# First layer's head in program order: three engines' queues fixed up to MoBA's queries, the second projection chunk in the scores' PSUM banks, the compression one chunk later

## The chip, the cores and the metric

One core of one Trainium2 chip runs the whole program. The metric is device time in microseconds (us) of one execution. The engines are TensorE (PE), VectorE (DVE), ScalarE (ACT) and GpSimd (POOL); SyncE (SP) issues nearly all DMAs. The profile is one execution in the hardware profiler; its times count from the first instruction of the program.

## The reference

Two decoder layers over 256 tokens of width 1024. A layer norms x, projects it with one wide matrix, feeds three token mixers (MoBA, NSA, FoX), gates and lifts their outputs, merges them and projects back onto x.

```python
h = rms_norm(x, norm_g)
proj = h @ w_in          # mq mk mv mz | nq kc vc ksl vsl kw vw ng nz | fq fk fv ff fz gl
q = apply_partial_rope(rms_norm(split_heads(mq, 6), ...), cos, sin)      # MoBA; the same for k
o_moba = moba_attention(q, k, split_heads(mv, 6))
k_cmp = nsa_compress(kc, gidx, cmp_pe[0], cmp_w1[0], cmp_w2[0])          # silu(flat @ w1) @ w2
v_cmp = nsa_compress(vc, gidx, cmp_pe[1], cmp_w1[1], cmp_w2[1])
o_nsa = nsa_attention(q, k_cmp, v_cmp, cmp_end, ksl, vsl, kw, vw, gates)
o_fox = fox_attention(q, k, v, log_f)
merged = g0 * (o_moba*silu(mz) @ w_up_moba) + g1 * (o_nsa*silu(nz) @ w_up_nsa) + g2 * (o_fox*silu(fz) @ w_up_fox)
return x + merged @ w_out
```

## The kernel before

**Weights.** All weights stream from HBM in tiles of up to 1024 columns (`chunk`, L229). A tile is loaded into one of six `st` buffers by SP (`load`, L246), then split into a high half `wh` (ScalarE, L262) and a low half `wl` (VectorE, L263), one of four buffers each (`wsp`). A dense product is three matmuls in reduced-width float: high by high, high by low, low by high (`mm3`, L286 to L289). `prefetch` and `part` (L265 to L280) emit the split of the tile four ahead of the one that is used next (AHEAD = 4). So a split waits for three things: its load, PE's release of the `wh` and `wl` four tiles back, and its place in ACT's and DVE's queues. A load waits for the `st` buffer six tiles back.

**Chunks of the projection.** In the order of use (ORDER, L1032): "a" (NSA's queries, compression tokens, slc keys and values), "mv", "b" (window keys and values, gates), then "w0" to "w3" (the compression's first matrix in four parts, two tiles of four 256 KB loads in all per part) strewn between "mq" and "mz", and so on. Every other chunk comes in two halves (mv0, mv1) of two tiles each.

**PSUM.** `pacc` has four banks: two row tiles of the chunk that is accumulated, two of the chunk that is evacuated. `pat` has three banks named "at", for transposes and later the scores; `po` has one.

**Order.** PE's order is written by hand: the program emits matmuls, and a planner's clock (`tick`, L199) advances by each matmul's estimated cost. Post-processing units are generators that yield the us after which their next part is due (`post_a` L685, `post_b` L712, `cmp_tokens` L733, `v_post`, `qk_post`); their instructions are emitted where the clock finds them due. On ACT, DVE, POOL and SP the framework's own scheduler orders instructions, by priority and estimated readiness. `first_blocks` (L373) chains the first ones by hand.

**The stage at issue** is `run` (L1079) for layer 0, from the first matmul of "a" to w3. `first_blocks` splits a's four tiles together with the first blocks of x; `mm_first` multiplies them; mv follows. Meanwhile x is loaded (L126), squared (L422), and `rsqrt` (L306) makes the row factor `rt` from the sums. All evacuations need rt: `post_a` evacuates kv and vsl (L442), squares the heads (L446, one `sq` buffer) and reduces (L447), makes the head factors, scales and ropes the heads (L511, L464 to L467), the slc keys (L520). `cmp_tokens` transposes kv on PE (L739), adds positions (`zf`, one buffer, L742) and splits the sum into Z (L748 on ACT, L749 on DVE); w0's matmuls (L773, L774) read Z. `rope_tables` (L426) and `cmp_zeros` (L751) are POOL's.

Of the kernel before, what the change touches and what calls it, by code (L numbers as in the profile page):

```python
# [9 lines left out]
F32 = mybir.dt.float32  # L10
# [8 lines left out]
NT = S // 128  # L19
# [74 lines left out]
def trunk(ctx, tc, x, w_in, b_gate, cmp_w1, w_up_moba, w_up_nsa, w_up_fox, w_out, gains_d, eye_d, x_t, small_d, row_d, out):  # L94
# [5 lines left out]
    LAG_T, LAG_C, LAG_A, LAG_F, LAG_Q = 3.5, 4.5, 11.0, 9.0, 10.0  # L100
    HEADS, STAG, SECOND, LAG_S, LAG_P, LAG_B, PV = 2, 2.0, 1.5, 4.5, 2.5, 3.0, 0.1
    ctx.enter_context(tc.manual_schedule(engines={mybir.EngineType.PE}))

    const = ctx.enter_context(tc.tile_pool(name="const", bufs=1))
    lay = ctx.enter_context(tc.tile_pool(name="lay", bufs=1))
# [54 lines left out]
    def late_consts():  # L160
        V.memset(ones1, 1.0)
        G.memset(zer, 0.0)
        for s in (0, 64):
            V.memset(gcol[s:s + 16, 0:12], 1.0)
# [12 lines left out]
    def after(i, others):  # L177

        for o in others:
            tc.add_manual_dep(i.ins, o.ins.name, nosync, reason="one table set after the other")  # L180
# [110 lines left out]
    def new_acc():  # L291
        return [pacc.tile([128, 512], F32, name="acc") for _ in range(NT)]
# [57 lines left out]
    def layer(l):  # L350
# [22 lines left out]
        def first_blocks():  # L373


            last = {}

            def put(e, i):
                after(i, [last[e]] if e in last else [])
                last[e] = i  # L380
            z = sh["z"][0][:, 0:256]
            put(V, V.memset(z, 0.0))
            ps = pat.tile([128, 512], F32, name="at")
            for _ in range(6):
                T.matmul(ps[:, 0:256], z[:, 0:128], z, start=True, stop=True)
            for k in range(KD):
                w_, i = parts[f"a{k // 4}"][k % 4]
                if i == 0:
                    room(w_)
                xt, h, lo = [a[:, k % 4, :] for a in (sh["xt"][k // 4], *sh["hT"][k // 4])]  # L390
                g = ngc[:, l * KD + k:l * KD + k + 1]
                wh, wl = split(w_, i * 512, i * 512 + 512)
                if k == 0:
                    put(V, V.tensor_scalar(h, xt, g, None, op0=ALU.mult))
                else:
                    put(A, A.activation(h, xt, AF.Copy, scale=g))
                put(A, wh())
                put(V, V.scalar_tensor_tensor(lo, xt, g, h.bitcast(F32), op0=ALU.mult, op1=ALU.subtract))
                put(V, wl())
            used[0] = 4  # L400

        def x_loads():

            sh["xt"] = [pgs.tile([128, 4, S], F32, name="xt", tag="page") for _ in range(2)]

            def xk(a, b):
                nc.sync.dma_start(sh["xt"][a // 4][:, a % 4:a % 4 + b - a, :], x_t[:, a:b, :])
            xk(0, 1)
            load(tiles[0], (nc.scalar, nc.sync))
            xk(1, 2)  # L410
            xk(2, 3)
            load(tiles[1], (nc.scalar, nc.sync))
            xk(3, 4)
            xk(4, 6)
            load(tiles[2], (nc.sync,))
            xk(6, 8)
            for w_ in tiles[3:6]:
                load(w_, (nc.sync,))

        def start_r():  # L420
# [20 lines left out]
        def evac(ps, t, col, n, dst):  # L441
            A.activation(dst, ps[t][:, col:col + n], AF.Copy, scale=sh["r"][:, t:t + 1])  # L442
# [6 lines left out]
        def head_factors(ss, nh):  # L449

            rr = sm.tile([128, NT, 8], F32, name="rr")[:, :, 0:nh]
            rsqrt(rr, ss[:, :, 0:nh], 1.0 / HD, (128, NT, nh))
            V.tensor_tensor(rr, rr, sh["r"][:, :, None].to_broadcast([128, NT, nh]), op=ALU.mult)
            return rr
# [70 lines left out]
        def new_ss():  # L525
            return sm.tile([128, NT, 8], F32, name="ss")
# [158 lines left out]
        def post_a():  # L685
            ps = sh["ps_a"]
            sh["nqT"] = lay.tile([128, 2, S], F32, name="nqT")
            sh["nqs"] = lay.tile([128, NH, S], F32R, name="nqs")
            for n in ("kh2", "kl2"):
                sh[n] = lay.tile([128, 2, S], F32R, name=n)  # L690
            sh["kv"] = lay.tile([128, NT, 128], F32, name="kv")
            sh["vsl"] = lay.tile([128, NT, HD], F32, name="vsl")
            ss = new_ss()
            for t in range(NT):
                evac(ps, t, 256, 128, sh["kv"][:, t, :])
                sumsq(ss, ps, t, 0, 4)
                sumsq(ss, ps, t, 384, 1, h0=4)
                evac(ps, t, 448, HD, sh["vsl"][:, t, :])
            rr = head_factors(ss, 5)
            qs = heads_scaled(ps, rr, 0, 4, "nq")  # L700
            ks = shared_scaled(ps, 384, rr, 4, "ns")
            yield LAG_A
            for t in range(NT):
                p3, g = q_cols(qs[t], sh["nqs"], t, 2, "nq")
                A.activation(sh["nqT"][:, :, t * 128:(t + 1) * 128], p3, AF.Copy, scale=g)
                yield 0.2
            yield 3.0
            for t in range(NT):
                shared_cols(ks[t], 0, t, "ns")
                yield 0.2  # L710
# [288 lines left out]
        def mm_out(parts, between):  # L999
# [18 lines left out]
            for t in range(NT):  # L1018
                for n in range(2):
# [9 lines left out]
        parts = {}  # L1029
        PROJ = {"a": (C_NQ, 512), "b": (C_KW, 396), "mq": (C_MQ, 384), "mk": (C_MK, 384), "mv": (C_MV, 384),  # L1030
                "mz": (C_MZ, 384), "fq": (C_FQ, 384), "fk": (C_FK, 384), "fv": (C_FV, 384), "fz": (C_FF, 390)}
        ORDER = ["a0", "a1", "mv0", "mv1", "b0", "w0", "b1", "mq0", "w1", "mq1", "w2", "mz0", "mz1", "w3",  # L1032
                 "mk0", "mk1", "fv0", "fv1", "fq0", "fq1", "fz0", "fz1", "fk0", "fk1"]

        def queue_loads():
# [13 lines left out]
        def mm(o, starts=None):  # L1049
            name = o[:-1]  # L1050
            if name == "w":
                return mm_w1(int(o[-1]), parts[o])
            n, h = PROJ[name][1], int(o[-1])
            if h == 0:
                sh["ps_" + name] = new_acc()
            dense(sh["ps_" + name], sh["hT"], parts[o], n, h)

        def mm_first(starts):
# [20 lines left out]
        def run(starts, following):  # L1079
            mm_first(starts)  # L1080
            if l == 0:
                mm("mv0")
                start_r()
                late_consts()
                rope_tables()
                ua = unit(post_a())
            else:
                start_r()
                rope_tables()
                ua = unit(post_a())  # L1090
                mm("mv0")
            cmp_zeros()
            uz = unit(cmp_tokens())
            mm("mv1")
            uv = unit(v_post("mv"))
            if l == 0:
                zero_lows()
                later_loads()
            mm("b0")
            finish(uz)  # L1100
            mm("w0")
            mm("b1")
            ub = unit(post_b())
            mm("mq0")
            mm("w1")
            mm("mq1")
            uq = unit(qk_post("mq"))
            mm("w2")
            mm("mz0")
            mm("mz1")  # L1110
            unit(z_post())
            mm("w3")
            uc = unit(cmp_post())
            hs = pairs(nsa_heads(0, "vsl"), [ua, uc])
            h2 = pairs(nsa_heads(1, "vw"), [ua, ub])
            hc = unit(cmp_heads(), [uc, ua], 1.5, HEADS)
            mm("mk0")
            mm("mk1")
            uk = unit(qk_post("mk"))
            hm = pairs(heads3("mq", "mk", "mv", 0, 0, False) + heads3("mq", "mk", "mv", 1, 0, False), [uq, uk, uv])  # L1120
            mm("fv0")
            mm("fv1")
            uv = unit(v_post("fv"))
            mm("fq0")
            mm("fq1")
            uq = unit(qk_post("fq"))
            mm("fz0")
            mm("fz1")
            uf = unit(fz_post())
            mm("fk0")  # L1130
            mm("fk1")
            uk = unit(qk_post("fk"))
            hf = pairs(heads3("fq", "fk", "fv", 0, 640, True) + heads3("fq", "fk", "fv", 1, 640, True),
                       [uq, uk, uv, uf])
            every = hs + h2 + [hc] + hm + hf
            for c in range(5):
                mm_gl(c, sh["gls"][c])
            finish(*every)
            g0, g1 = unit(gate_out(0)), unit(gate_out(1))
            unit(gate_sig(0))  # L1140
            unit(gate_sig(1))
            mm_gl(5, sh["gls"][5])
            unit(gate_sig(2))
            mm_up(0, sh["ups"][0], {0: [g0], 1: [g1]})
            m0 = unit(merged_T(0))
            mm_up(1, sh["ups"][1], {})
            m1 = unit(merged_T(1))
            finish(m0)
            state["sigs"] = sigs
            mm_out(sh["outs"], following)  # L1150
            finish(m1)
# [38 lines left out]
```

## Time and profile before

| | |
|---|---|
| median of 3 runs | 513.04 us (512.91 to 515.11) |
| the profiled execution: its time | 516.09 us |
| the profiled execution: its span, first to last instruction | 514.3 us |
| busy share of the span: PE, DVE, ACT, POOL | 98%, 78%, 65%, 12% |
| granted TensorE clock, mean over the span | 0.993 of full |
| HBM read, mean rate | 90.71 MB, 178 GB/s |

The page gives busy shares, slices and the chain of work that ended last; answers of the trace go closer. A time line has one row for one instruction or several equal ones: start, duration, engine, line, operation, output<-inputs, shape, count, and in brackets the idle time of the engine before it with what ended it. "PEclk" is the granted clock, 1.00 being 2.4 GHz and 0.50 being 1.2 GHz.

### The profile page before, as it was taken

How to read it: one execution, taken by the hardware profiler on the slowest of the kernel's cores; microseconds unless marked ns; L12 is line 12 of the kernel's file. 1: busy time of each engine (PE TensorE's matmuls, PEld its weight loads, DVE VectorE, ACT ScalarE, POOL GpSimd, SP SyncE). 2: the span in 40 equal slices, each digit the busy share in tenths (PEclk: the TensorE clock that was granted, in tenths of full speed). 3: DMA queues.
4: the chain of work that ended last, by engine and by line, in shares of the span. 5: the costliest groups of instructions: out<-in, count | busy, mean ns of one | idle time of the engine just before them, and what ended most of it. 6: DMA issues, size and time to landing. Idle time of an engine off the chain costs nothing.

```text
span 514.3 us, 8253 instructions
## 1 busy us (share of the span) xinstructions
PE 503.3 (98%) x2822; PEld 450.2 (88%) x2822; DVE 401.7 (78%) x846; ACT 334.1 (65%) x645; POOL 62.5 (12%) x84
## 2 busy tenths in 40 slices
PE   9969999999999999999999999999999999999997
PEld 7869999999888888888889999999988888888886
DVE  6587988689987556988586998768898855698953
ACT  5676767877576776563366887767756866655440
POOL 3520121000120004023300000000011000042300
PEclk9988999999999999999999999999999999999999
DMA  8998896565575335565647799656457453537502
GB/s 280 315 226 221 214 281 181 144 202 159 156 240 161 111 117 164 159 207 169 182 106 213 186 245 279 185 155 179 141 187 238 143 137 115 164 117 227 183 7 82
DMA packets 58802, 92.31 MB, mean 179 GB/s; under 512 B 3964, under 2 KB 33288, under 8 KB 58760
## 3 DMA queue, kind: packets, MB, share of 16 engines
q1 hardware_dynamic: 56736, 89.67, 60.3%
q10 hardware_dynamic: 2024, 2.12, 1.2%
q8 instruction: 22, 0.36, 0.3%
q14 instruction: 20, 0.16, 0.1%
HBM read 90.71 MB, written 1.06 MB: 178 GB/s over the span
## 4 chain that ended last, share of the span: by engine, by line
PE 84%; DMA 6%; ACT 5%; DVE 3%; issue 1%; ACTq 0%; SPq 0%; DVEq 0%
PE acc L287 23%; PE acc L289 22%; PE acc L288 22%; DMA st<-in_w_in_dram 6%; PE at L584 2%; ACT wh L262 2%; DVE wl L263 2%; PE at L570 2%; PE at L571 2%; PE at L336 1%; PE o L592 1%; PE o L596 1%; PE o L594 1%; PE o L774 1%; PE o L773 1%
## 5 line engine op out<-in xcount | busy, mean ns | idle before, releaser
L263 DVE TENSOR_TENSOR wl<-st,wh 128x1024 fp32r<-128x1024 f32 (+4 forms) x180 | 200.5, 1121 | 56.0 <-ACT wh L262 54.3
L262 ACT ACTIVATE wh<-st 128x1024 fp32r<-128x1024 f32 (+4 forms) x180 | 170.7, 953 | 96.2 <-PE acc L289 70.8
L287 PE MATMUL acc<-wh,hT 128*128 128x512 f32 (+4 forms) x560 | 218.2, 390 | 2.1 <-ACT v L442 2.1
L288 PE MATMUL acc<-wl,hT 128*128 128x512 f32 (+4 forms) x560 | 204.0, 364 | 0.8 <-DVE wl L263 0.8
L289 PE MATMUL acc<-wh,lT 128*128 128x512 f32 (+4 forms) x560 | 204.0, 364 | 0.0
L289 PEld LDWEIGHTS acc<-wh,lT 128*128 128x128 f32 x560 | 106.1, 189 | 11.0
L287 PEld LDWEIGHTS acc<-wh,hT 128*128 128x128 f32 x560 | 106.7, 191 | 9.7 <-ACT v L442 2.5
L288 PEld LDWEIGHTS acc<-wl,hT 128*128 128x128 f32 x560 | 106.8, 191 | 8.0 <-DVE wl L263 1.6
L579 ACT ACTIVATE p<-p,nm 128x128 f32<-128x128 f32 x80 | 35.5, 445 | 20.9 <-DVE nm L577 20.8
L947 POOL TENSOR_TENSOR z<-z,tmp 128x512 f32<-128x512 f32 x8 | 12.9, 1646 | 108.6 <-ACT tmp L944 108.6
L287 PE MATMUL acc<-wh,qkT 128*128 128x512 f32 x64 | 25.6, 400 | 0.0
L289 PE MATMUL acc<-wh,qkT 128*128 128x512 f32 x64 | 25.0, 391 | 0.0
L288 PE MATMUL acc<-wl,qkT 128*128 128x512 f32 x64 | 25.0, 390 | 0.0
L985 POOL TENSOR_TENSOR mg<-mg,tmp 128x512 f32<-128x512 f32 x8 | 15.8, 1996 | 51.5 <-DVE tmp L984 51.5
L584 PE MATMUL at<-ident,p 128*128 128x128 f32 x120 | 19.8, 274 | 0.3
L933 DVE SCALAR_TENSOR_TENSOR gl<-acc,rt,tmp 128x512 f32<-128x512 f32 x24 | 17.0, 742 | 1.4 <-PE o L596 1.1
L584 PEld LDWEIGHTS at<-ident,p 128*128 128x128 f32 x120 | 15.0, 146 | 2.5 <-ACT qkT L498 0.6
L774 PE MATMUL o<-wl,Z 128*63 128x256 f32 x64 | 15.3, 278 | 1.9 <-DVE wl L263 1.9
L577 DVE CUSTOM_DVE_ANT_0 p<-at,tabs 128x128 f32<-128x128 f32 (+1 forms) x56 | 17.0, 350 | 0.1
L446 ACT ACTIVATE sq<-acc,rt 128x384 f32<-128x384 f32 (+2 forms) x28 | 13.6, 487 | 3.7 <-PE acc L289 3.2
L586 ACT ACTIVATE pt<-at 128x384 f32<-128x384 f32 x20 | 9.7, 483 | 9.8 <-PE at L584 9.4
L588 DVE COPY pt<-at 128x384 f32<-128x384 f32 x20 | 11.0, 552 | 5.6 <-PE at L584 5.4
(238 smaller groups left out, 694.2 us busy)
## 6 DMA issues: line engine op xcount, KB each, us to landing
st<-in_w_in_dram SPq DMA_DIRECT2D x52, 512.0 KB, 3.6
st<-in_w_in_dram SPq DMA_DIRECT2D x56, 384.0 KB, 4.2
st<-in_cmp_w_dram SPq DMA_DIRECT2D x32, 256.0 KB, 4.9
st<-in_w_out_dram SPq DMA_DIRECT2D x16, 512.0 KB, 4.4
st<-in_w_in_dram SPq DMA_DIRECT2D x8, 396.0 KB, 6.3
st<-in_w_in_dram SPq DMA_DIRECT2D x8, 390.0 KB, 3.1
tmp<-in_b_gate_dram SPq DMA_DIRECT2D x12, 256.0 KB, 4.2
st<-in_w_up_moba_dram SPq DMA_DIRECT2D x4, 512.0 KB, 3.5
```

The lines of the kernel that those rows point to most:

```text
L262: return (lambda: A.activation(h, s_, AF.Copy), lambda: V.tensor_tensor(lo, s_, h.bitcast(F32), op=ALU.subtract))
L263: lambda: V.tensor_tensor(lo, s_, h.bitcast(F32), op=ALU.subtract))
L287: T.matmul(ps, sh, wh, start=first, stop=False)
L288: T.matmul(ps, sh, wl, start=False, stop=False)
L289: T.matmul(ps, sl, wh, start=False, stop=last)
L446: A.activation(sq, ps[t][:, col:col + nh * HD], AF.Square, scale=sh["r"][:, t:t + 1])
L577: V.tensor_tensor_reduce(out=u, in0=sp, in1=add[t], scale=-SCALE, scalar=BIG, op0=ALU.add, op1=ALU.min, accum_out=nm)
L579: exps.append(A.activation(u, u, AF.Exp, bias=nm, scale=-1.0, accum_out=rsum[:, t, hb:hb + 1]))
L584: T.transpose(pts[:, s * 128:(s + 1) * 128], p[:, s * 128:(s + 1) * 128], ident)
L774: T.matmul(U, st, lo, start=False, stop=i == CL - 1)
L933: V.scalar_tensor_tensor(sh["gl"][t][b][:, n * 512:(n + 1) * 512], ps[t], sh["r"][:, t:t + 1], bg, op0=ALU.mult, op1=ALU.add)
L985: (G if b == 1 else V).tensor_tensor(m, m, tmp, op=ALU.add)
```

## The change

1. A second guard, `front`, fixes the order of ACT, DVE and SP to the order in which the program emits, from the start to mq0 of layer 0. The hand-made chain in `first_blocks` goes.
2. `x_loads` also issues mv1's two loads, before the small tables and x. Two prefetches are emitted around `start_r`.
3. mv of layer 0 accumulates in two "at" banks instead of two `pacc` banks.
4. In layer 0 the order of chunks is b0, b1, mq0, w0, mq1, w1, mz0, w2, mz1, w3; b and mq0 come ahead of the compression's first part. `cmp_tokens` becomes a unit after mv1 and is due in b0. The loads of two tables (`later_loads`) come after mq0, when the guard ends.
5. `post_a` yields four times more in layer 0, so that its parts are spread over mv and b0.

```diff
+    front = ExitStack()
+    front.enter_context(tc.manual_schedule(engines={mybir.EngineType.Activation, mybir.EngineType.DVE, mybir.EngineType.SP}))
...
         def first_blocks():
-            last = {}
-
-            def put(e, i):
-                after(i, [last[e]] if e in last else [])
-                last[e] = i
...
-            for w_ in tiles[3:6]:
+            for w_ in tiles[3:8]:
                 load(w_, (nc.sync,))
...
             ss = new_ss()
+            pause = 0.0 if l else 2.0
             for t in range(NT):
                 evac(ps, t, 256, 128, sh["kv"][:, t, :])
                 sumsq(ss, ps, t, 0, 4)
                 sumsq(ss, ps, t, 384, 1, h0=4)
                 evac(ps, t, 448, HD, sh["vsl"][:, t, :])
+                if l == 0:
+                    yield pause
             rr = head_factors(ss, 5)
+            if l == 0:
+                yield pause
             qs = heads_scaled(ps, rr, 0, 4, "nq")
+            if l == 0:
+                yield pause
             ks = shared_scaled(ps, 384, rr, 4, "ns")
...
-        ORDER = ["a0", "a1", "mv0", "mv1", "b0", "w0", "b1", "mq0", "w1", "mq1", "w2", "mz0", "mz1", "w3",
+        ORDER = ["a0", "a1", "mv0", "mv1"] + (
+            ["b0", "w0", "b1", "mq0", "w1", "mq1", "w2", "mz0", "mz1", "w3"] if l else
+            ["b0", "b1", "mq0", "w0", "mq1", "w1", "mz0", "w2", "mz1", "w3"]) + [
...
-                sh["ps_" + name] = new_acc()
+                sh["ps_" + name] = new_acc() if l or name != "mv" else [
+                    pat.tile([128, 512], F32, name="at") for _ in range(NT)]
...
             mm_first(starts)
             if l == 0:
-                mm("mv0")
+                prefetch(8)
                 start_r()
+                prefetch(9)
                 late_consts()
                 rope_tables()
                 ua = unit(post_a())
+                mm("mv0")
+                cmp_zeros()
+                mm("mv1")
+                uv = unit(v_post("mv"))
+                uz = unit(cmp_tokens())
+                zero_lows()
+                mm("b0")
+                mm("b1")
+                ub = unit(post_b())
+                mm("mq0")
+                front.close()
+                later_loads()
+                finish(uz)
+                mm("w0")
+                mm("mq1")
+                uq = unit(qk_post("mq"))
+                mm("w1")
+                mm("mz0")
+                mm("w2")
+                mm("mz1")
+                unit(z_post())
+                mm("w3")
             else:
...
```

Under `else` the former order stands for layer 1; before, both layers used it, with `zero_lows` and `later_loads` ahead of b0 in layer 0.

## Rows read from the trace of the kernel before

**Rows 1.** The page's busy times, and its chain that ended last by engine
```profile
PE 503.3 (98%) x2822; PEld 450.2 (88%) x2822; DVE 401.7 (78%) x846; ACT 334.1 (65%) x645; POOL 62.5 (12%) x84
...
PE 84%; DMA 6%; ACT 5%; DVE 3%; issue 1%; ACTq 0%; SPq 0%; DVEq 0%
```

**Rows 2.** PE's waits, whole span: who waited for whom: us in total, times, longest
```profile
PE acc L287 <- ACT v L442: 2.1, 1, 2.1
PE o L774 <- DVE wl L263: 1.9, 1, 1.9
...
PE acc L288 <- DVE wl L263: 0.8, 2, 0.6
PE at L475 <- ACT nqT L705: 0.4, 1, 0.4
```

**Rows 3.** PE's time line: mv0's start and three waits (columns as told above)
```profile
17.09 0.33 PE L287 MATMUL acc<-wh,hT 128*128 128x384 f32 x1
...
26.59 0.33 PE L739 MATMUL at<-ident,kv 128*128 128x128 f32 x1 [0.97 <-ACT kv L442]
...
30.14 0.70 PE L287 MATMUL acc<-wh,hT 128*128 128x396 f32 x1 [2.15 <-ACT v L442]
...
39.04 0.33 PE L774 MATMUL o<-wl,Z 128*63 128x256 f32 x1 [1.90 <-DVE wl L263]
```

**Rows 4.** Stretches: length, busy us (instructions) of PE, PEld, DVE, ACT, POOL; PEclk; DMA share; GB/s
```profile
6.00:17.00 11.00, 11.00 (x50) 9.09 (x49) 9.48 (x19) 8.54 (x17) 0.38 (x1) 1.00 1.04 368
17.00:21.30 4.30, 4.30 (x27) 4.16 (x25) 0.87 (x3) 3.17 (x7) 4.24 (x17) 1.00 1.01 353
21.30:27.90 6.60, 5.02 (x27) 4.22 (x26) 5.07 (x9) 4.20 (x10) 1.94 (x3) 1.00 1.11 206
30.14:32.90 2.76, 2.76 (x8) 2.76 (x9) 2.05 (x6) 1.93 (x5) 0.00 (x0) 0.50 1.08 205
40.10:43.00 2.90, 2.90 (x10) 2.89 (x10) 2.43 (x3) 0.79 (x1) 0.00 (x0) 0.50 0.82 222
50.00:60.00 10.00, 9.80 (x66) 9.00 (x65) 9.16 (x24) 7.84 (x17) 1.32 (x3) 1.00 0.73 200
```

**Rows 5.** ACT's time line: x's second square and the reading of its sum
```profile
19.24 1.06 ACT L422 ACTIVATE om<-x 128x1024 f32<-128x1024 f32 x1 [0.20 <-DMA x<-in_x_dram]
20.21 0.18 ACT L422 ACTIVATION_READ_ACCUMULATOR om<-x 128x1 f32 x1
```

**Rows 6.** DVE's time line: the last steps of the row factor
```profile
22.14 0.56 DVE L317 SCALAR_TENSOR_TENSOR rs_a<-rs_v,rs_y 128x2 f32<-128x2 f32 x1
22.74 0.62 DVE L318 TENSOR_TENSOR rs_a<-rs_a,rs_y 128x2 f32<-128x2 f32 x1
...
24.15 0.15 DVE L319 SCALAR_TENSOR_TENSOR rt<-rs_a,rs_y 128x2 f32<-128x2 f32 x1
```

**Rows 7.** POOL's time line: the zeros of Z
```profile
20.14 3.21 POOL L756 CAST Z<-zer 64x512 fp32r<-64x512 f32 x4
```

**Rows 8.** DVE's groups by form, 0 to 70 us: shapes, count | busy us, mean ns | idle before
```profile
L263 DVE TENSOR_TENSOR wl<-st,wh 128x768 fp32r<-128x768 f32 x13 | 12.3, 960 | 2.0 <-ACT wh L262 2.0
L263 DVE TENSOR_TENSOR wl<-st,wh 128x1024 fp32r<-128x1024 f32 x8 | 9.7, 1227 | 3.5 <-ACT wh L262 3.5
...
L263 DVE TENSOR_TENSOR wl<-st,wh 128x792 fp32r<-128x792 f32 x4 | 3.9, 982 | 0.6 <-ACT wh L262 0.6
...
L749 DVE TENSOR_TENSOR Z<-zf,Z 64x256 fp32r<-64x256 f32 x4 | 2.5, 622 | 0.7 <-ACT rs_y L315 0.6
...
L317 DVE SCALAR_TENSOR_TENSOR rs_a<-rs_v,rs_y 128x10 f32<-128x10 f32 x1 | 0.2, 171 | 0.0
```

**Rows 9.** PE's time line: w1's start, mq1's start, the first instruction after w3
```profile
50.65 0.28 PE L773 MATMUL o<-wh,Z 128*63 128x256 f32 x1
...
52.48 0.34 PE L287 MATMUL acc<-wh,hT 128*128 128x384 f32 x1
...
69.73 0.27 PE L475 MATMUL at<-ident,qn 128*128 128x128 f32 x1
```

More of the change, by code (lines that the diff above doesn't have):

```diff
@@ L373, in first_blocks @@
         def first_blocks():
-            last = {}
-            def put(e, i):
-                after(i, [last[e]] if e in last else [])
-                last[e] = i
             z = sh["z"][0][:, 0:256]
-            put(V, V.memset(z, 0.0))
+            V.memset(z, 0.0)
             ps = pat.tile([128, 512], F32, name="at")
@@ L393, in first_blocks @@
                 if k == 0:
-                    put(V, V.tensor_scalar(h, xt, g, None, op0=ALU.mult))
+                    V.tensor_scalar(h, xt, g, None, op0=ALU.mult)
                 else:
[L396 to L399, printed above, removed]
+                    A.activation(h, xt, AF.Copy, scale=g)
+                wh()
+                V.scalar_tensor_tensor(lo, xt, g, h.bitcast(F32), op0=ALU.mult, op1=ALU.subtract)
+                wl()
             used[0] = 4
@@ L1091, in run @@
                 mm("mv0")
[L1092 to L1112, printed above, removed]
+                cmp_zeros()
+                uz = unit(cmp_tokens())
+                mm("mv1")
+                uv = unit(v_post("mv"))
+                mm("b0")
+                finish(uz)
+                mm("w0")
+                mm("b1")
+                ub = unit(post_b())
+                mm("mq0")
+                mm("w1")
+                mm("mq1")
+                uq = unit(qk_post("mq"))
+                mm("w2")
+                mm("mz0")
+                mm("mz1")
+                unit(z_post())
+                mm("w3")
             uc = unit(cmp_post())
```

## The prediction, made before the changed kernel ran

> **What bounds the kernel now.** The page's busy shares come first: TensorE is busy 98% of the span, and the chain that ended last is 84% PE [rows 1]. So only time in which PE idles, or runs at half clock, can be won. The list of PE's waits says for whom [rows 2], the time line of PE where [rows 3]: nearly all lie in the first 60 us. They are 0.6 us for the low half of mv1's first tile at 22 us; 1.0 us for the kv evacuation at 26 us; 2.15 us before b0, for ScalarE to empty the second chunk's two PSUM banks; 1.9 us in w0 for a low half. After the last two PE runs at half clock, 1.2 GHz: granted 0.50 over 30.14 to 32.90 and 40.10 to 43.00 [rows 4]. The low stretches are some 3.0 and 3.4 us long, so they cost 1.5 and 1.7 us. All in all 5.6 + 0.2 (the second, small wait of two on wl in [rows 2]) + 3.2 = 9.0 us, or 1.8% of the span, is the most this stage can give. Behind it stands a second bound: VectorE is busy 9.16 of 10 us at 50 to 60 us [rows 4]. It makes every weight's low half, so it can't run far ahead.
>
> **What is removed, cover by cover.** (a) mv goes to two of the three "at" banks, so b0 finds the second pair of accumulator banks empty: the 2.15 us wait and its half clock (1.5) go. (b) The kv transposes move from mv1 into b0, so the 1.0 us wait goes. (c) mv1's loads are issued before the small tables and x, so wh and wl of mv1 no longer come behind x's squares: 0.6 us go. (d) w0 goes behind b0, b1 and mq0, and so do its four 256 KB loads and the two table loads; in the trace all packets slow down when these are in flight: 206 GB/s at a DMA share of 1.11 over 21.3 to 27.9, against 368 GB/s before 17 us [rows 4]. b's and mq0's loads then land by some 28 us. That is early enough to cost nothing, and worth nothing where a load isn't last.
>
> **What is late next.** ACT, DVE and SP now issue in the order in which the program emits; a wait of one instruction holds all behind it. I follow that order with durations from the rows, from the last load of x on. A step is the duration of the row, less some 0.1 us where independent work on one engine overlaps.
>
> *The row factor rt.* In before x's second square starts with its data at 19.24 [rows 5]. Two tiles more (0.79 MB at the 353 to 368 GB/s of [rows 4]: 2.1 us) now lie ahead of x: square at 21.3, its sum at 22.5. From that sum to rt before took 20.39 to 24.30, with two 0.9 us low halves between [rows 5, 6, 8]; without them 2.0 us. So rt comes at 24.5, hardly later than before. In this I keep VectorE's tiny steps at the 0.56 and 0.62 us of [rows 6]: POOL's zero casts, 20.14 to 23.35 [rows 7], ran beside them, and alone such a step takes 0.17 [rows 8]. The casts stand behind the rope tables, which wait for the row load, also some 2 us later, so they overlap again. Bounds: 0.85 us less if they don't, 0.6 more if the third small step is held too. The Trainium skill, "SBUF — State Buffer", section "Who interferes with whom", says that a VectorE instruction with two SBUF inputs contends with a GpSimd instruction that reads SBUF, the second being held till the first ends. It speaks against this change, which moves both chains together; by it each of three steps could be held for a whole cast of 0.8 us, and rt would come at 25.5 and the time at 513.7, inside the forecast's own range.
>
> *rt to b0's second low half.* b0's first tile (wl 0.98), the constants (0.2), then for both row tiles: kv, square, reduce, square, smaller reduce, vsl. There is one square buffer, so ACT and DVE alternate: per row tile a reduce and two squares of 0.3 to 0.5 us in turn, 3.5 us for both. wh and wl of b0's second tile stand behind them: 1.0 + 1.0 with the handover. Together 5.8 us, to 30.3. PE starts mv0 at 17.09 [rows 3]; mv0 and mv1 are 96 matmuls at a pitch of 0.173, 8.3 us, and b0's first tile 12 at 0.179: PE is through at 27.6, and waits: **2.7 us**.
>
> *To the compression tokens.* In DVE's order: head factors 1.55 (seven steps of 0.17 to 0.2 [rows 8] with ACT between), wl of b1's first tile 0.98, four scaled heads with rope 1.4, wl 0.9, wl of mq0's first tile 0.87, slc keys with rope 1.2. That makes 6.7, to 37.0. Then zf 0.42, high halves on ACT 0.65, low halves 0.62 [rows 8], twice, since zf has one buffer: 4.8 us, to 41.8. Only then come wh and wl of mq0's second tile: 42.8. PE, slowed by half clock after the first wait, has reached that tile by 40: it waits **2.8 us**; without the slow stretch 4.
>
> *To mq1.* wl of w0's two tiles 2.3; the window keys' two sums of squares, factors, scaling and gates 3.8 with ACT's turns; wl of mq1's first tile 0.96: 7.1 us, to 49.95. PE finishes mq0, w0 and two transposes at 48.8 (with half clock to 46): it waits **1.1 us**. This third wait is what sets the time; the two before it, and their half clock, vanish in it.
>
> **The sum.** In before mq1 starts at 52.48 and w3 ends at 69.73, 17.25 us; w1, now behind mq1, takes 1.83 and transposes that now fall here 0.35 [rows 9]: 19.4 us. After: 49.95 + 19.4 = 69.4. So w3 ends 0.3 us earlier, and from there PE is the bound to the end (0.4 us of waits in the remaining 445 us [rows 2]). Of 9.0 us, nearly all comes back as three waits behind ACT's and DVE's order. The span is 514.3 and the profiled execution 516.09 us, 1.8 around it; the median of the runs is 3.05 below that execution (0.6%). A change of 0.3 in the span I take off the median: **512.7 us**.
>
> Bounds. The chain from rt to mq1 has some 60 small steps; ±1.5 us. If the third wait is above what keeps the clock up, half clock follows: +1.6. In before a wait of 0.97 kept it and 1.90 did not [rows 3, 4]; mine, 1.1, is nearer the first, so I take nothing. The order after the guard ends is the planner's; it cost 0.2 us of PE in before [rows 2]: 0 to 3.1 (below). Moving rope tables, zero tiles and POOL's work costs nothing while it ends before 37 us: it starts with the row load near 18.6, takes 6.7 us, ends at 25.3. The two table loads moved behind mq0 serve heads after 70 us: zero, up to 1.5 us of DMA if they go ahead of w1.
>
> **Rivals.**
> 1. *Slower: DVE's debt falls due at w2.* At 50 us DVE has not yet done the query columns (1.9 us of nqs) and mq's head work (sums 1.1, factors 1.35, scaling and rope 2.4), which in before lay in its idle time or later. If that is placed ahead of w2's low halves, PE waits at w2 for 2.5 us, then 0.6 for the next ones: 512.7 + 3.1 = 515.8; with half clock after it 517.4. For it: 92% busy DVE [rows 4]. Against: the planner kept low halves first in before (0.2 us of PE). It decides from some 1.5 us of debt not covered at 59 us.
> 2. *Faster: the banks and loads are what counts.* The order written in the program is nearly the one that ran, ACT and DVE alternate without the idle that I count (3.5 us on DVE between rt and 37 us), and only the wait behind rt is left: 9.0 − 2.7 gives 506.7; half of it 509.7. For it: each wait removed is plain in [rows 2]. Against: the low halves' places in the program order can be counted. The Trainium skill, "Perfetto Trace Analysis", section Matmuls, has independent groups rotate through PSUM banks so that one's evacuation overlaps the next's matmuls; by it b0's wait goes and nothing replaces it. The 2.15 us of [rows 3] agree that this wait is a bank's; whether a wait replaces it no run here shows yet.
> 3. *It doesn't do what it says:* the guard leaves ACT's and DVE's order as the planner had it; only banks and w0's place change. That saves the b0 and w0 waits with half clock, 7.25 us, less what DVE then lacks, some 2 to 4: 508 to 511.
>
> **How the numbers follow.** The forecast, 512.7, own range 510.5 to 515.2, 0.57. Rival 1 0.19; rival 2 0.16; rival 3 0.08. About 0.5%, 2.6 us, is what a measurement of this kernel can tell from no change. Faster by that (below 510.5): rival 2 and most of 3, 0.22. Slower (above 515.6): most of rival 1 with half clock, 0.17. Within: 0.61. The range 507.5 to 516.5 leaves out the best half of rival 2 and rival 1's worst, some 0.16.
>
> **What would show it.** In the changed kernel: b0's first matmul without a wait; kv and rt near 24.5; a wait of PE in b0's second tile for wl near 30, in mq0's second near 43, before mq1 near 50; w3's end near 69.4; granted clock 0.5 behind the first two. I'm wrong if DVE's low half of mq0's second tile comes before 40 us (then rival 2), or if PE waits over 1 us at w2 (rival 1).

## The result, and the profile after

The changed kernel takes 517.37 us (median of 5 runs, 516.97 to 517.91) beside 513.32 us for the kernel before on the same chip (5 runs, 512.91 to 515.11): a ratio of 1.0059, 95% interval 1.0034 to 1.0084. On a second chip, with more runs of the kernel before, it is 517.59 beside 514.71: 1.0053 (1.0033 to 1.0073). The first two medians lie 4.05 us apart, but the kernel before scatters by over 3 us and has only five runs there; the ratios of both sessions say 2.7 to 3.0 us. So it is slower by some 2.8 us, where 0.3 us faster was forecast, and 517.4 lies above the range of 507.5 to 516.5.

The profiled execution took 517.15 us, span 515.4. PE's waits over the whole span (waiting engine and line, releaser: total, times, longest), to be read against [rows 2]:

```profile
PE acc L291 <- DVE wl L266: 3.1, 5, 1.4
PE acc L290 <- ACT wh L265: 2.8, 1, 2.8
PE at L383 <- DVE z L380: 1.2, 1, 1.2
PE o L779 <- DVE wl L266: 0.9, 1, 0.9
PE at L473 <- ACT nqT L710: 0.4, 1, 0.4
```

The waits for v and kv are gone; in their place stand waits for high and low halves. Where they lie shows PE's time line of the changed kernel (start, duration, engine, line, output<-inputs, shape, count, idle before with releaser):

```profile
28.95 0.45 PE L291 MATMUL acc<-wl,hT 128*128 128x396 f32 x1 [0.57 <-DVE wl L266]
...
41.10 0.44 PE L290 MATMUL acc<-wh,hT 128*128 128x384 f32 x1 [2.83 <-ACT wh L265]
42.10 0.44 PE L291 MATMUL acc<-wl,hT 128*128 128x384 f32 x1 [0.55 <-DVE wl L266]
49.51 0.44 PE L291 MATMUL acc<-wl,hT 128*128 128x384 f32 x1 [1.40 <-DVE wl L266]
...
57.75 0.33 PE L473 MATMUL at<-ident,kn 128*128 128x128 f32 x1 [0.24 <-DVE kl L504]
...
69.57 0.33 PE L779 MATMUL o<-wl,Z 128*63 128x256 f32 x1 [0.93 <-DVE wl L266]
...
70.46 0.34 PE L290 MATMUL acc<-wh,hT 128*128 128x384 f32 x1
71.20 0.44 PE L291 MATMUL acc<-wl,hT 128*128 128x384 f32 x1 [0.41 <-DVE wl L266]
```

The first three places (b0's, mq0's second tile, mq1) are those of the forecast; the last two, w3 and mk0, are not in it. w3 ends at 70.46, against 69.73 in [rows 9]. The five-us stretches (stretch, its length, busy PE, PEld, DVE, ACT, POOL, then granted clock, DMA share, GB/s):

```profile
25.00:30.00 5.00, 4.34 (x23) 3.70 (x23) 2.36 (x8) 3.35 (x10) 0.00 (x0) 1.00 0.74 196
30.00:35.00 5.00, 4.84 (x28) 4.48 (x27) 4.83 (x13) 2.65 (x5) 2.11 (x3) 1.00 0.89 240
35.00:40.00 5.00, 3.27 (x19) 2.95 (x17) 3.35 (x11) 2.39 (x4) 0.66 (x3) 1.00 0.83 237
40.00:45.00 5.00, 3.35 (x12) 3.09 (x13) 4.29 (x7) 4.30 (x11) 0.00 (x0) 0.78 0.29 78
45.00:50.00 5.00, 3.60 (x24) 3.21 (x23) 4.01 (x16) 4.74 (x11) 0.65 (x3) 0.88 0.66 184
```

VectorE, the engine that is owed the low halves, is busy only 2.36, 3.35 and 4.01 of 5 us in three of these. It idles because its next instruction in the written order waits for ScalarE: in its time line, behind the first square's reduce, and again at the tokens:

```profile
26.15 0.42 DVE L445 TENSOR_REDUCE ss<-sq 128x4 f32<-128x256 f32 x1 [0.61 <-ACT sq L444]
26.95 0.22 DVE L445 TENSOR_REDUCE ss<-sq 128x1 f32<-128x64 f32 x1 [0.38 <-ACT sq L444]
27.91 0.98 DVE L266 TENSOR_TENSOR wl<-st,wh 128x792 fp32r<-128x792 f32 x1 [0.74 <-ACT wh L265]
...
35.98 0.42 DVE L747 TENSOR_TENSOR zf<-at,tabs 128x256 f32<-128x256 f32 x1
37.12 1.29 DVE L754 TENSOR_TENSOR Z<-zf,Z 64x256 fp32r<-64x256 f32 x2 [0.72 <-ACT Z L753]
38.44 0.42 DVE L747 TENSOR_TENSOR zf<-at,tabs 128x256 f32<-128x256 f32 x1
39.56 1.25 DVE L754 TENSOR_TENSOR Z<-zf,Z 64x256 fp32r<-64x256 f32 x2 [0.70 <-ACT Z L753]
41.08 3.31 DVE L266 TENSOR_TENSOR wl<-st,wh 128x768 fp32r<-128x768 f32 x3 [0.26 <-ACT wh L265]
```

### The profile page after: what moved, and what is told of

Same layout as the page of the kernel before. It is cut to its first block, busy times and chain, and to the rows that moved or that the text cites. A ratio compares the mean times of both kernels' runs of the same rounds, so it can differ in the third digit from the quotient of the medians.

```text
span 515.4 us, 8259 instructions
## 1 busy us (share of the span) xinstructions
PE 503.0 (98%) x2822; PEld 448.6 (87%) x2822; DVE 402.3 (78%) x846; ACT 334.7 (65%) x645; POOL 61.7 (12%) x84
## 3 DMA queue, kind: packets, MB, share of 16 engines
HBM read 90.71 MB, written 1.06 MB: 178 GB/s over the span
## 4 chain that ended last, share of the span: by engine, by line
PE 81%; ACT 6%; DVE 6%; DMA 4%; issue 2%; SPq 0%; DVEq 0%; ACTq 0%
PE acc L290 23%; PE acc L292 21%; PE acc L291 21%; DVE wl L266 3%; ACT wh L265 3%; PE at L582 2%; PE at L568 2%; PE at L569 2%; PE at L339 1%; PE o L590 1%; DMA st<-in_w_in_dram 1%; PE o L592 1%; PE o L594 1%; PE at L473 1%; DMA x<-in_x_dram 1%
## 5 line engine op out<-in xcount | busy, mean ns | idle before, releaser
L290 PE MATMUL acc<-wh,hT 128*128 128x512 f32 (+4 forms) x544 | 211.8, 389 | 2.9 <-ACT wh L265 2.8
L291 PE MATMUL acc<-wl,hT 128*128 128x512 f32 (+4 forms) x544 | 198.0, 364 | 3.1 <-DVE wl L266 3.1
L292 PE MATMUL acc<-wh,lT 128*128 128x512 f32 (+4 forms) x544 | 198.1, 364 | 0.0
L291 PEld LDWEIGHTS acc<-wl,hT 128*128 128x128 f32 x544 | 103.1, 190 | 10.7 <-DVE wl L266 4.5
L290 PEld LDWEIGHTS acc<-wh,hT 128*128 128x128 f32 x544 | 103.1, 189 | 10.6 <-ACT wh L265 3.6
L292 PEld LDWEIGHTS acc<-wh,lT 128*128 128x128 f32 x544 | 102.5, 188 | 11.0
L778 PE MATMUL o<-wh,Z 128*63 128x256 f32 x64 | 16.0, 288 | 0.1
```

The costliest lines, as they stand in the source:

```text
L290: T.matmul(ps, sh, wh, start=first, stop=False)
L291: T.matmul(ps, sh, wl, start=False, stop=False)
L292: T.matmul(ps, sl, wh, start=False, stop=last)
L778: T.matmul(U, st, h, start=i == 0, stop=False)
```

## Experiments

In each, "before" is the kernel before on the same chip in the same session; ratios are to it, with 95% intervals. The theory to be tested is that of the forecast in short: the written order on ScalarE and VectorE, not PE, sets the time up to mq1.

**Where the kernel before scatters.** Unchanged, three times more: e1 with runs of its own, then two single executions.

> The kernel before, unchanged, for the clock of each execution. The profiled execution of before took 516.09 us, its runs 513.3 in the median. Theory (clock): the two half-clock stretches after PE's waits in the first 45 us (1.5 and 1.7 us) happen only in some executions; those with mean granted clock near 1.000 take 512.9 to 513.3, those with 0.993 to 0.995 take 515 to 516. Rival (profiling): the profiled execution is slower for another reason, and time and clock do not go together; then executions of the same clock differ by 2 us or more.

It took 514.65 us (12 runs, 513.57 to 516.85), ratio 0.9994 (0.9978 to 1.001). Runs with the same mean clock differ by 3 us (at 0.996: 513.38 to 516.43), so the mean clock doesn't sort them.

> A trace of the kernel before, to see where its executions (513.4 to 517.0 us) differ. Both traces so far are of executions near the upper end (516.09 and 516.85); they have PE waits of 1.9 and 3.1 us in w0 for a low half. Theory (w0's four loads land late in some executions): an execution under 515 us has a wait in w0 under 1 us and no half clock at 40 to 45 us; b0's wait stays between 1.7 and 2.2 us. Rival (the difference lies behind 70 us): the same waits in w0 in an execution under 515 us.

> As e11_before_look: one more trace of the kernel before, with the same two readings.

These two took 514.05 and 513.42 us. PE's time line at w0's low half and at w3's end, with the stretch between (columns as above), of e11 and then of e12:

```profile
38.53 0.33 PE L774 MATMUL o<-wl,Z 128*63 128x256 f32 x1 [0.41 <-DVE wl L263]
...
40.00:45.00 5.00, 5.00 (x31) 4.92 (x30) 4.12 (x6) 3.31 (x9) 0.00 (x0) 1.00 1.02 274
...
67.70 0.49 PE L475 MATMUL at<-ident,qn 128*128 128x128 f32 x3
```

```profile
37.87 0.33 PE L774 MATMUL o<-wl,Z 128*63 128x256 f32 x1 [1.56 <-DVE wl L263]
...
40.00:45.00 5.00, 5.00 (x31) 4.91 (x31) 3.95 (x7) 3.58 (x9) 0.00 (x0) 1.00 1.09 301
...
67.06 0.49 PE L475 MATMUL at<-ident,qn 128*128 128x128 f32 x3
```

The half clock behind w0's wait, which [rows 4] show from 40.10 to 43.00, isn't there. The wait itself is smaller than 1.90 in both, though in e12 not below the 1 us expected. From the end of w0's wait to the end of w3 it takes 29.17 us in e11 and 29.19 in e12, but 30.69 in the execution of [rows 3] and 31.95 in e1 (38.57 to 70.52), where the clock was 0.50 from 38 to 44 us: 1.5 and 2.8 us of the scatter are this half clock, which the mean over the whole span doesn't show. The end of the wait itself varies from 37.87 (e12) to 39.04; 0.6 us of that is x's second square, at 18.67 in e12 and at 19.24 to 19.33 in the others. Late loads of w0, the theory of e11, no trace shows as the cause: in all four the low half that PE waits for stands right behind Z's low halves on VectorE. And the rest of the kernel is constant: the execution's time less the start of the transposes behind w3 is 516.09 − 69.73 = 446.36 in [rows 9], 516.85 − 70.52 = 446.33 in e1, 514.05 − 67.70 = 446.35 and 513.42 − 67.06 = 446.36 here. All 3.4 us of scatter between these four lie ahead of w3's end.

**The changed kernel again.**

> The changed kernel once more, beside the kernel before on another chip and with more runs. The first comparison gave 517.37 against 513.32, 4.05 us slower, while the two traces place every instruction behind 112 us only 1.03 to 1.07 us later than before. Theory A (the trace carries the change; the rest of the 4 us was the share of before's few executions that came out short): after minus before is 1 to 2.5 us, about 1.0025 as a ratio, and single executions of either kernel scatter over 3 us. Theory B (the change costs about 4 us and one trace of before isn't typical): 3.5 to 4.5 us again, a ratio of about 1.0075. Late landmarks of its trace: within 0.5 us of those of the first trace of after under both.

517.59 us (6 runs, 517.39 to 518.13), 1.0053 (1.0033 to 1.0073): 2.9 us, a little above theory A's bound and below B's. Its profiled execution took 518.13 us; x's second square starts at 21.60, 1.00 later than in the first trace, and what stands behind it is 0.92 to 1.01 later: mq0's wait ends at 42.10, mq1's at 50.52, w3 at 71.38. Unlike the kernel before, it scatters by only 1.2 us over both chips (516.97 to 518.13).

**The banks and no more.** On the kernel before:

```
-                sh["ps_" + name] = new_acc()
+                sh["ps_" + name] = new_acc() if l or name != "mv" else [
+                    pat.tile([128, 512], F32, name="at") for _ in range(NT)]
```

> The kernel before with one edit: mv of layer 0 accumulates in two scores' banks. Theory (the bank is a wait of its own): b0's 2.15 us wait goes, 1.5 to 2.2 us gained, 511 to 512 us; the wait in w0 stays. Rival (DVE and ACT set the pace behind rt): b0 then waits for its low half or w0 waits longer, and the time stays within 0.5 us of 513.3.

515.81 us (12 runs), 1.0023 (1.0008 to 1.0037): 1.2 us slower, which neither side had. PE's waits:

```profile
PE o L774 <- DVE wl L263: 4.7, 1, 4.7
...
PE o L773 <- DVE Z L749: 0.7, 1, 0.7
```

b0's wait is gone, and w0's has grown from 1.90 to 4.70, ending at 39.17, where it ended at 39.04 before. The removed wait came back whole, one chunk later, and PE ran at half clock behind it (0.58 over 40 to 45).

**Without the guard.** The changed kernel, the two lines of `front` removed and the hand-made chain of `first_blocks` put back.

> The changed kernel without the guard: ACT, DVE and SP are ordered by the planner again (the hand-made chain of the first blocks is back), all else as changed: mv in the scores' banks, w0 behind mq0, mv1's loads ahead of x, post_a in parts. Theory (the written order costs): the low half of mq0's second tile comes near 37 to 38 us, before the compression's second half, so the 3.4 us wait in mq0 and the 1.4 us wait before mq1 go or shrink below 1 us in all: 508 to 511 us. Rival (the chunks' new order or the later x costs): 516 to 518 as the changed kernel.

515.68 us (12 runs), 1.0021 (1.0007 to 1.0034), not the 508 to 511 of the theory: of the change's 0.53 to 0.59% the guard is some 0.35, a difference of ratios from two sessions with intervals of ±0.13 to ±0.25% each. The rest of the change isn't a gain either; what its 0.2% is made of no run separates. PE still waits 1.12 and 0.55 us at 43 to 44, and 0.73, 0.93 and 0.45 at w3 and mk0.

**mz's evacuation at w3.** In the changed kernel ScalarE idled 2.90 us ahead of it, with the high half of w3's second tile queued behind it, though that tile's load had landed at 65.0:

```profile
62.76 1.06 ACT L265 ACTIVATE wh<-st 128x1024 fp32r<-128x1024 f32 x1 [0.65 <-DMA st<-in_cmp_w_dram]
66.72 0.58 ACT L440 ACTIVATE z<-acc,rt 128x384 f32<-128x384 f32 x1 [2.90 <-PE acc L292]
67.21 1.05 ACT L265 ACTIVATE wh<-st 128x1024 fp32r<-128x1024 f32 x1
```

The edit ties it behind mk0's first high half:

```
-                evac(sh["ps_mz"], t, 0, 384, sh["z"][t][:, 0:384])
+                i = evac(sh["ps_mz"], t, 0, 384, sh["z"][t][:, 0:384])
+                if l == 0:
+                    after(i, [parts["mk0"][0][0]["made"][0]])
```

> The changed kernel with one edit: ScalarE's two evacuations of mz stand behind the high half of mk0's first tile in ACT's queue. In the profile of the changed kernel ACT sat idle 2.9 us at 63.8 to 66.7 before the first of them, with the high half of w3's second tile behind it; PE then waited 0.93 us in w3 and 0.41 in mk0. Theory (place in ACT's queue): both waits go, 1.2 to 1.4 us gained, 516.0 us. Rival (VectorE's debt or the load of that tile, which landed at 65.0): the waits stay above 0.8 us in all, 517 us or more.

516.43 us (6 runs), 1.0034 (1.002 to 1.0047). That high half now starts at 64.82, and w3's wait of 0.93 is gone; mk0's stays (0.39). The three earlier waits stand unchanged (0.57, 2.86 with 0.55, 1.42).

> Without the guard (the planner orders ScalarE, VectorE and the loads from the start, first_blocks chained by hand as before) and with mz's evacuation tied behind the high half of mk0's first tile. Theory (two separate costs): e2_no_guard had 0.73, 0.93 and 0.45 us of waits at w3 and mk0, behind a z evacuation that stood 3.6 us on ScalarE; they go here, as they did in e4_z_late, so it is 1.0 to 2.0 us faster than e2_no_guard's 1.0021 of before: a ratio of 0.998 to 1.0003. PE's waits near 44 (1.1 and 0.6 us) and near 52 (0.5 and 0.5) stay. Rival (the end is set by something behind w3, and waits at w3 are made up later): ratio stays at 1.002. If both kernels of this pair are beaten by anything so far, it is by this one.

516.13 us (12 runs), 1.0024 (1.001 to 1.0038): without the guard no gain shows (e2 has 1.0021). There ScalarE idles 4.45 us ahead of a head's columns instead, and w3 and mk0 wait 0.57, 0.93 and 0.45 as before. The theory of one separate cost held only inside the guarded order.

**Moving work along the written order.** First the tokens, behind mq0's second low half: `yield 2.0 if l else 4.5` in `cmp_tokens`.

> The changed kernel with cmp_tokens due 4.5 instead of 2.0 us after mv1 in layer 0, so that zf and Z's low halves (4.8 us of VectorE with its waits for ScalarE) stand behind the low half of mq0's second tile instead of ahead of it. Theory (VectorE's and ScalarE's order is the bound up to mq1; the second wait vanishes in the third): PE's 2.83 and 0.55 us near 41 go, but Z is some 1 us later, so w0 waits for it about 1.5 us, mq1's first low half is still ready at 49 to 50 us, the third wait grows or stays, and w3's end and the time stay within 0.7 us of after's (ratio to before as e5_after_again's, within 0.0015). Rival (each wait of PE is its own loss): 2.5 to 3.4 us faster than after, w3's end near 67.5.

520.92 us (6 runs), 1.0122 (1.0101 to 1.0142), 3.3 us slower than the changed kernel; neither side had that. PE's time line:

```profile
43.88 0.30 PE L778 MATMUL o<-wh,Z 128*63 128x256 f32 x1 [0.92 <-issue]
45.09 0.33 PE L779 MATMUL o<-wl,Z 128*63 128x256 f32 x1 [0.91 <-DVE wl L266]
48.96 0.44 PE L290 MATMUL acc<-wh,hT 128*128 128x384 f32 x1 [1.50 <-ACT wh L265]
52.05 0.69 PE L291 MATMUL acc<-wl,hT 128*128 128x384 f32 x1 [2.65 <-DVE wl L266]
```

mq0's wait is gone as planned, but mq1's grew to 4.15 us, and half clock follows it (0.64 over 50 to 55, 0.68 over 55 to 60) with no longer wait behind it to absorb it (w3 waits 0.93, as in the changed kernel). x landed late as well (second square at 22.10).

Then `post_b` behind w0 instead of ahead of mq0:

> The changed kernel with post_b started behind w0 instead of behind b1. It takes the window keys' two reduces, factors, scaling and gates (43.1 to 48.9 us on VectorE in after) out from ahead of mq1's low halves. Theory (third wait sets the time): mq1's 1.40 us wait goes and nothing replaces it until w2, so it is 1.0 to 1.5 us faster than after; w3's end near 69.2. Rival (VectorE's debt only moves): the waits at w2, w3 and mk0 (0.24, 0.93 and 0.41 in after) grow by what was saved, and the time stays within 0.5 us of after's.

517.96 us (6 runs), 1.0066 (1.0042 to 1.0091). mq1's wait is gone, and new ones stand behind it: 0.51 at 67.14 for a head and 0.69 at 69.29 in w3, where the 0.93 stays (at 70.56). w3 ends at 71.40, as in e5 (71.38). The rival holds in the time; that it is VectorE alone isn't shown, since the 0.69 is a wait for ScalarE's high half.

Then x one tile earlier: `tiles[3:7]` in `x_loads`, `start_r` ahead of the prefetch.

> The changed kernel with one of mv1's two loads (0.39 MB, some 1.05 us) issued behind x instead of ahead of it, and the squares of x ahead of the split of that tile. Theory (x's landing is passed on one to one: after and e5_after_again differ by 1.00 us in x's second square, 20.60 and 21.60, and by 0.97 to 0.99 us at every landmark behind it): the second square at 19.5 to 20.7, rt 1 us earlier than in after for the same scatter, a new wait of PE in mv1 of 0.3 to 1.0 us for that tile's low half, and the time 0.8 to 1.3 us below e5_after_again's 517.6. Rival (the wait for the low halves behind rt is set by ScalarE and VectorE alone, not by x): within 0.4 us of 517.6.

517.64 us (6 runs), 1.006 (1.0039 to 1.008): no gain. VectorE's time line shows why:

```profile
22.13 0.46 DVE L322 SCALAR_TENSOR_TENSOR rt<-rs_a,rs_y 128x2 f32<-128x2 f32 x1
22.51 2.26 DVE L266 TENSOR_TENSOR wl<-st,wh 128x768 fp32r<-128x768 f32 x2
...
24.93 0.42 DVE L445 TENSOR_REDUCE ss<-sq 128x4 f32<-128x256 f32 x1
```

rt is 0.87 earlier than in the changed kernel (22.13 for 23.00). But the tile put behind x now has its low half between rt and the first reduce: two low halves, 2.26 us, for one of 0.97. The reduce comes 0.41 later than in the changed kernel (24.52 there), mq0's and mq1's waits end 0.42 later (41.52, 49.93), and w3 0.37. Even this loss is passed on nearly one to one.

All three edits (e4, e8, e9) together:

> e9_x_earlier, e4_z_late and e8_window_keys_later in one kernel. Theory (what is left of the change's cost sits in these three places, and they add up): with x's landing held equal e4 gained 1.1 us and e8 0.9 us against after, e9 some 1.0: 3.0 us in all, 514.6, a ratio to before of 1.000. Rival (VectorE is the one bound, and each edit only moves its debt): not more than 1.3 us below after's 517.6, a ratio above 1.003, with waits of 1 us or more left at w3 and mk0.

518.2 us (6 runs), 1.0076 (1.0049 to 1.0103): the rival. A wait of 1.56 us at 57.70 is new, and w3 waits 0.68 and 0.93.

**The idle time inside the order.** What is left is VectorE's idle time where it and ScalarE hand single buffers back and forth. In layer 0 the squares of `post_a` and the two zf go to the four "tmp" buffers, idle at this stage, and both zf are added ahead of their splits:

```
-            sq = wk.tile([128, 384], F32, name="sq", bufs=1)[:, 0:nh * HD]
+            sq = (wk.tile([128, 512], F32, name="tmp", bufs=4) if l == 0 and ps is sh["ps_a"] else
+                  wk.tile([128, 384], F32, name="sq", bufs=1))[:, 0:nh * HD]
...
+            zfs = [add_pe(v) for v in range(2)] if l == 0 else None
```

> The changed kernel; in layer 0 the squares of post_a and the two zf go into the four tmp buffers, which are idle at this stage, and both zf are added ahead of the splits. Order, loads, banks and waits of PE's program stay. Theory (the cost is VectorE's idle time inside the written order, where it and ScalarE hand one buffer back and forth; each us of that chain is passed on one to one): between rt and mq1's first low half the chain is 1.2 us shorter at the squares and 0.9 us at the tokens; PE's waits near 41 and 49 move 1.3 to 2.2 us earlier, the time falls by 1.5 to 2.2 us against 517.6, to 515.4 to 516.1. Rival (the chain is bound by the work of the two engines, not by the buffers): below 0.7 us, as with e9_x_earlier.

> The same edit on the kernel before, where the planner fills the gaps with low halves. Theory: PE's waits for kv (0.97) and for v (1.73 to 2.15) come from the same single square buffer; they shrink by 0.5 to 1 us together, and the time falls by 0 to 1.0 us (a ratio of 0.998 to 1.000): VectorE is already 4.1 to 5.0 us busy of 5 there, so less is idle to win than in the changed kernel. Rival (those waits are worth their full length): 1.5 us or more faster.

> e13_more_buffers with e4_z_late's edit. If the two costs are separate (the chain ahead of mq1, and the z evacuation at w3) they add: 1.0 us below e13, 514.4 to 515.1, level with the kernel before. If the edit at w3 only moves VectorE's debt: within 0.4 us of e13.

e13 took 516.66 us (6 runs, 515.76 to 518.3), 1.006 (1.0044 to 1.0076): by the ratio no gain at all over the changed kernel's 1.0053 to 1.0059. e14, the edit on the kernel before, took 514.31 (11 runs), 1.0006 (0.9992 to 1.002): no difference, as its theory had it, though not for its reason, since PE's waits for kv and v hardly shrank (0.88 and 2.05). e15 took 514.01 (12 runs), 1.0004 (0.9991 to 1.0017): level with the kernel before. It is 2.65 us below e13, where 1.0 was expected, and by the ratios some 2.5 us below the changed kernel; the medians differ by 3.6, but come from two chips on which the kernel before differs by 0.94. PE's time line of e13, with two stretches, and then the same of e15:

```profile
38.38 0.45 PE L290 MATMUL acc<-wh,hT 128*128 128x384 f32 x1 [1.21 <-ACT wh L265]
...
46.78 0.44 PE L291 MATMUL acc<-wl,hT 128*128 128x384 f32 x1 [2.23 <-DVE wl L266]
...
45.00:50.00 5.00, 3.22 (x14) 3.19 (x15) 4.87 (x10) 2.50 (x4) 0.65 (x3) 0.81 0.61 183
50.00:55.00 5.00, 5.00 (x32) 4.96 (x32) 3.54 (x7) 3.87 (x8) 0.00 (x0) 0.85 1.08 264
...
67.30 0.33 PE L784 MATMUL o<-wh,Z 128*63 128x256 f32 x1 [0.29 <-ACT wh L265]
68.56 0.33 PE L785 MATMUL o<-wl,Z 128*63 128x256 f32 x1 [0.93 <-DVE wl L266]
70.20 0.44 PE L291 MATMUL acc<-wl,hT 128*128 128x384 f32 x1 [0.44 <-DVE wl L266]
```

```profile
38.54 0.44 PE L289 MATMUL acc<-wh,hT 128*128 128x384 f32 x1 [1.71 <-ACT wh L265]
...
46.95 0.44 PE L290 MATMUL acc<-wl,hT 128*128 128x384 f32 x1 [1.39 <-DVE wl L266]
...
40.00:45.00 5.00, 5.00 (x26) 4.91 (x26) 3.70 (x12) 4.29 (x15) 0.00 (x0) 0.66 0.81 217
...
67.37 0.44 PE L290 MATMUL acc<-wl,hT 128*128 128x384 f32 x1 [0.39 <-DVE wl L266]
```

In both, the waits at mq0 and mq1 end 2.6 to 2.7 us earlier (38.4 and 46.8 for 41.1 and 49.5), and 2.5 earlier counted from rt, which came up to 0.2 sooner in them. That is more than the 1.3 to 2.2 expected; on VectorE of e13, 1.5 us of it lie at the squares and 1.1 at the tokens, so the size of this term is shown. What it is worth isn't: e13 gains nothing by it, e15 2.5 us together with the z evacuation. In e13 PE came to mq1 at full clock, waited longer, and ran at half clock behind it (0.81 over 45 to 50, 0.85 over 50 to 55: 0.19 + 0.15 of 5 us, 1.7 us); in e15 half clock fell ahead of mq1 (0.66 over 40 to 45), and the wait there took it up. The other difference, 1.3 us of waits at w3 and mk0, is the z evacuation again. So the two edits don't simply add up, and the half clock's place decides 1.7 us. Why e13's half clock fell behind and e15's ahead, with the same order up to there, no run here settles.

## Why the prediction was wrong

Taken against the constant rest, 446.35 us behind w3's end, the error divides as follows:

| | us |
|---|---|
| forecast | 512.7 |
| its own end of w3, 69.4, plus 446.35 | 515.75 (+3.05) |
| end of w3 at 70.46 | 516.81 (+1.06) |
| what follows w3 takes longer (mk0's wait of 0.41) | 517.15 (+0.34) |

517.15 is the profiled execution; the median is 517.37. The second trace of the changed kernel, e5, has the same remainder (518.13 − 71.38 = 446.75, for 446.69 in the first); its w3 ends 0.92 us later, after x's second square came 1.00 later.

**The step that failed most** is the last one of the sum: "A change of 0.3 in the span I take off the median". All landmarks were computed in absolute time, and 69.4 was compared with the 69.73 of one execution that took 516.09 us. Beside e11 and e12 that execution had 1.5 us of half clock behind w0's wait, and the wait ended 0.5 and 1.2 us later: 2.0 and 2.7 of the 3.05 (no execution right at the median was traced). The chain that I forecast contains neither w0's wait nor its half clock. To take its gain off the median was to remove them twice. By its own w3 end the forecast was 515.75, and against the typical end of w3 in the kernel before, 514.7 − 446.35 = 68.35, it was a loss of 1 us.

**rt and the first two waits: right in kind.** rt came at 23.46 (forecast 24.5). x's square was 0.7 earlier, and the small steps, taken at 0.56 and 0.62, were 0.16, the rt step alone 0.46, with the casts beside them. b0's second low half was done at 28.9 (forecast 30.3, with a wait of 2.7; the trace has 0.57, and e5 1.16 with 0.57), and the clock stayed at 1.00, where I had half clock. The terms named for that stretch add up to 6.7 us; the "5.8" holds only with 0.9 of overlap that isn't listed. It took 5.4. zf started at 35.98 (37.0). mq0's second low half was due at 42.1 (42.8), with PE waiting 3.4 (2.8), and half clock followed, as forecast.

**The third wait: right within 0.44 us.** It ended at 49.51 (49.95) after 1.40 us (1.1), with no half clock behind it. That it came so close is luck in part: rt was 1.0 us early, and the chain from rt to mq1 0.6 us longer than forecast. That what happens to PE ahead of it vanishes in it is shown: from the start of the rt step to the end of mq1's wait it takes 26.51 us in the changed kernel and 26.52 in e5, whose wait in b0 is 1.16 us longer; and 23.99 in e13 and 23.97 in e15, which has half clock ahead of mq1 where e13 has none. That this wait alone sets the time isn't so: e8 took it away and gained nothing.

**The tail: a term mis-sized.** "The order after the guard ends is the planner's ... 0 to 3.1": I took 0. It was 0.24 + 0.93 + 0.41 = 1.58. From mq1's wait to w3's end it took 20.95 us for the 19.4 forecast, 1.17 of it the first two of these. Rival 1 had the debt at w2 through VectorE; it fell due at w3 through ScalarE's queue, and e4 took 1.0 us of it back. Within the guarded order this is shown; e6 shows that it isn't general.

**Where the change's cost sits.** By e2, the guard costs some 0.35% of the 0.55. By e15, without the single buffers inside its order and with the z evacuation moved the loss is gone; how it divides between the two stays open, since alone the first gained nothing (e13) and the second 1.0 us (e4), and half clock takes 1.7 us in e13. VectorE's busy time between 25 and 50 us doesn't measure it: it is 18.83 in the changed kernel, 21.11 in e13 and 20.97 in e15, but in the kernel before, too, it is 18.78 (e1), 19.55 (first trace), 21.05 and 21.31 (e11, e12).

**Rival 2** (banks and loads count): e3 refutes it for the banks. The Trainium skill, "Perfetto Trace Analysis", section Matmuls, has rotating banks overlap one group's evacuation with the next's matmuls. The trace agrees so far: b0 starts without a wait. What bounded the stage came next in line. **Rival 3** (the guard changes nothing): VectorE's idle rows above refute it, and e2, where without the guard the waits lie elsewhere. Its own sum was off too: 513.04 − 7.25 + 2 to 4 is 507.8 to 509.8, not "508 to 511".

## What to carry to other kernels

Find the landmark behind which all executions take the same time, and read it in several executions before one trace is made the zero of a sum; a gain computed from one execution's waits mustn't be taken off a median of others in which these waits are shorter. When a hand-written order replaces a planner, list the places where two engines hand a single buffer back and forth: a planner may fill them with other work (e14: nothing to win), a fixed order idles there (2.5 us of chain up to mq1 in e13 and e15; worth 2.5 us of time in e15, together with the z evacuation, and nothing in e13). A wait of a 98% busy engine is worth what the next engine in line leaves of it: e3 removed 2.15 us, and the next wait grew by 2.8.

## What the runs showed of the hardware that I had not expected

**Half clock doesn't follow from a wait's length alone.** Behind 1.73 us (e1, at 29.83) the clock stayed at 1.00; behind 1.74 (e11, at 29.79) it was 0.50 from 29 to 35. Behind 1.56 (e12, in w0) it stayed, behind 1.11 and 0.57 (e7, near 30) it fell to 0.66 over 30 to 35. So it can't be forecast here from the wait alone. What it costs depends on what follows: 6 us of it in e11 came ahead of w0's wait, which was only 0.41 there, for 3.09 in e1 (it ended at 38.53 and 38.57).

**VectorE's small steps beside GpSimd's casts.** In the changed kernel:

```profile
21.47 3.36 POOL L761 CAST Z<-zer 64x512 fp32r<-64x512 f32 x4
...
22.61 0.16 DVE L320 SCALAR_TENSOR_TENSOR rs_a<-rs_v,rs_y 128x2 f32<-128x2 f32 x1 [0.51 <-ACT rs_y L319]
22.80 0.16 DVE L321 TENSOR_TENSOR rs_a<-rs_a,rs_y 128x2 f32<-128x2 f32 x1
23.00 0.46 DVE L322 SCALAR_TENSOR_TENSOR rt<-rs_a,rs_y 128x2 f32<-128x2 f32 x1
```

Two of three steps beside the casts take 0.16 us, as they do alone; only one takes longer. In the kernel before, both steps beside them did (0.56 and 0.62, [rows 6]). The Trainium skill, "SBUF — State Buffer", section "Who interferes with whom", has such steps held until the cast ends; the trace agrees for at most one in three here, and for at most both in [rows 6].

**The landing of x scatters.** With the same list of loads ahead of it, its second square started at 20.60, 21.60, 21.05, 21.81, 22.10, 20.36 and 20.45 us in the seven traces of guarded kernels that load it so (first trace, e5, e4, e8, e7, e13, e15).
